# A hybrid decoder step on one core: a write-after-read order across two names of one SBUF stretch, VectorE for urgent GpSimd work, another order of the seven products of a pair, and two figures of the planner

## The chip, the core and the metric

The kernel runs on one core of one Trainium2 chip. The metric is the device time of one execution in microseconds. An execution of the kernel before takes 1107.15 us (median of three: 1103.31, 1107.15 and 1110.06).

## What is computed

Two decoder layers run over 512 prompt tokens and 8 sample tokens of 1024 channels. A layer is an input projection, three kinds of token mixing (window attention, a gated recurrence, causal pooling), an output projection with a residual and a LayerNorm, and then a feed-forward block with a residual and a second LayerNorm:

```
u = x @ w_in            # 1024 -> mixed widths, attention / recurrence / pooling
x = LayerNorm(alpha * x + concat(A, B, C) @ w_out)
x = LayerNorm(alpha * x + relu(x @ w_ff1)^2 @ w_ff2)     # 1024 -> 4096 -> 1024
```

The outputs are the last hidden states of both token groups and the updated caches.

## The kernel before

**Tiles.** The tokens are worked on in two halves: half A has 256 prompt tokens, half B has the other 256 and the 8 sample tokens (264 columns). Activations lie with channels on the partitions, in eight chunks `m` = 0 to 7 of 128 channels. Every float32 matmul is done as three matmuls on pieces of reduced width (hi by hi, lo by hi, hi by lo), so each operand has two tiles: `xh`, `xl` for the layer's input, `hh`, `hl` for the hidden values of the feed-forward block, and a high and a low half in each of the seven weight slots `w`. In the listings `xh_113`, `xl_115`, `hh_0_124`, `hl_0_125`, `y_0_92` are half A's, `xh_114`, `xl_116`, `hh_0_126`, `hl_0_127`, `y_0_94` half B's. A product of 128 output channels over 1024 inputs is 24 matmuls.

**Weights.** SyncE issues loads of 1 MB into two buffers `raw` in turn. Each holds the weights of two products. ScalarE casts the high half (`CAST w<-raw`), VectorE subtracts it to get the low half (`w<-raw,w`), and then the buffer may be loaded again. All waits of SyncE's loads are in the order of its queue.

**Planner.** The kernel text only records operations in a `Plan`; `Plan.order` (L225) then list-schedules all of them with estimated durations and due times (`rank`), and each engine issues its work in that order. An operation recorded with `either` (L338) may go to VectorE or GpSimd, decided in `pick` (L257): another engine than the first named takes it under the rules at L265 to L271. `cost` (L174) gives a load its bytes, and `dma_free` (L252) is the time from which the planner takes the DMA rings to be free. Dependences are by tile and region (`add`, L124). The framework below then puts in the semaphore waits, by its own view of which memory an instruction reads and writes.

**The shared stretch.** One stretch of SBUF, 8384 floats in each partition, is known by two names: `over_f` (float32) and `over_r` (the type for the matmuls), with `plan.alias` mapping the second to the first (L346 to L348). By `over_f` it holds rotating work lines of the attention and norm stages (`place`, L349), among them the zero-padded keys `KZ`, which two GpSimd memsets clear at the start of each layer (`layer_start`, L786), and the bias line of the last norm, loaded from `in_ln_b` (`Norm.prepare`, L1183). By `over_r` it holds the sums of input tiles T1 to T4 of the pairs, which fill the whole stretch.

**Feed-forward.** It runs in passes of eight hidden chunks: passes 0 to 3 for half A, 1 to 4 for half B. In a pass, `f1` products make hidden chunks (relu, square, `hh`, `hl`), then `f2` products add to the running sum `y`. Three chunk pairs of passes 2 and 3 and two of pass 1 are done for both halves together by `do_pair` (L1429): seven block products p1 to p7 of 12 matmuls each give two chunks for both halves, in place of eight; each reads T1 to T4 (`over_r`) or `xh`, `xl`, and goes to a PSUM bank `s`, `t` or `mm`. `close` makes a hidden tile from the finished sums: VectorE add into `ra`, VectorE relu and square into `rb`, ScalarE cast into `hh`, VectorE subtract into `hl`. The products are recorded in the order p1, p6, p7, p2, p4, p5, p3, and the tiles close in the order A m, A m+1, B m+1, B m. After the last pair of a pass come half A's `f2` products, then half B's; each reads all eight hidden tiles of its half, m = 7 last. There are six such ends of pair groups, three in each layer.

**Norms.** `Norm.chunk(m)` (L1206) runs as each chunk of `y` is finished: it adds the chunk to `acc` (chunks 3 and 7 name VectorE first, the others GpSimd), and after chunk 3 a matmul with `onesm` gives the shift (`x<-acc,onesm`), after chunk 7 the mean, by the same kind of matmul.

Of the kernel before, what the change touches and what calls it, by code (L numbers as in the profile page):

```python
# [19 lines left out]
ADD, SUB, MUL, MAX, MIN = ALU.add, ALU.subtract, ALU.mult, ALU.max, ALU.min  # L20
# [41 lines left out]
class Plan:  # L62
# [3 lines left out]
    def __init__(self, tc):  # L66
        self.tc = tc
        nc = tc.nc
        self.engs = {"V": nc.vector, "S": nc.scalar, "G": nc.gpsimd, "T": nc.tensor, "P": nc.sync}
        self.ops = []  # L70
        self.writes, self.reads = {}, {}
        self.rings, self.psum = {}, set()
        self.alias, self.large = {}, False


    def tile(self, pool, shape, dt, tag, bufs, name, psum=False):
# [47 lines left out]
    def add(self, first, *others):  # L124
# [19 lines left out]
        for a, w in [(a, False) for a in ins] + [(a, True) for a in outs]:  # L144
            nm = self.alias.get(a.name, a.name)
            if a.space == bass.MemoryType.DRAM:
                continue
            r = self.region(a)
            wl, rl = self.writes.setdefault(nm, []), self.reads.setdefault(nm, [])

            def hit(q):
                return q[0] < r[1] and r[0] < q[1] and any(x < d and c < y for x, y in q[2] for c, d in r[2])
            for q, o in wl:
                if hit(q):
                    deps.add(o)
            if w:
                for q, o in rl:
                    if hit(q):
                        deps.add(o)

                def inside(q):
                    return r[0] <= q[0] and q[1] <= r[1] and all(any(c <= x and y <= d for c, d in r[2]) for x, y in q[2])
                wl[:] = [x for x in wl if not inside(x[0])]
                rl[:] = [x for x in rl if not inside(x[0])]
                wl.append((r, op))
            else:
                if nm in self.psum:
                    deps.update(o for _, o in rl if o.eng != eng or len(o.alts) + len(op.alts) > 2)
                rl.append((r, op))
        deps.discard(op)  # L170
        op.deps = deps
        return op

    def cost(self, op, method, outs, ins, args, kw):  # L174
# [10 lines left out]
        if method == "dma_start":  # L185
            b = 4
            for k in out.shape:
                b *= k
            op.bytes = b
            op.dur = 1.0 if op.eng == "G" else 0.5  # L190
        elif op.eng == "T":
            if method == "transpose":
# [32 lines left out]
    def order(self):  # L225
# [23 lines left out]
            if not o.deps:  # L249
                release(o)  # L250
        free = {e: 0.0 for e in pool}
        cur_set, dma_free, late = None, 0.0, -nxt_pe  # L252
        held = {e: 0.0 for e in pool}
        other = {"V": "G", "G": "V"}
        done = []
# [1 line left out]
        def pick(e):  # L257
# [6 lines left out]
            for est, o in found:  # L264
                if est <= t + WINDOW or len(o.alts) > 1:  # L265
                    start = max(free[e], est)
                    if e != o.eng:
                        if e == "G":
                            if o.rank + late - start < o.alts[e][1] + MARGIN:
                                continue  # L270
                        elif max(free[o.eng], est) <= start + BUSY:  # L271
                            continue
                    if est > t + WINDOW:
                        continue
# [48 lines left out]
def trunk_kernel(ctx, tc, x_prompt, x_sample, cache_k, cache_v, state_h, state_conv, state_pool,  # L323
# [1105 lines left out]
    def do_pair(l, p, c):  # L1429
# [29 lines left out]
            V.tensor_tensor(lo[:, mm], q, hi[:, mm].bitcast(F32), SUB)  # L1459
        p1 = mul(0, wa, 0, xf, 0, 264, (j, "a"))  # L1460
        S.copy(out=e1, in_=p1)
        p6 = mul(1, wb, 4, sums["T2"], 0, 264, (j, "b"))
        V.tensor_tensor(u2, e1, p6, ADD)
        p7 = mul(0, wc, 0, sums["T3"], 0, 264, (j, "c"))
        V.tensor_tensor(u3, u2, p7, ADD)
        p2 = mul(2, wa, 4, xf, 4, 256, (j, "a"))
        close(0, m, 0, e1, p2)
        p4 = mul(1, wc, 4, sums["T4"], 0, 256, (j, "c"))
        close(0, m + 1, 1, u3, p4)
        p5 = mul(0, wb, 0, sums["T1"], 0, 264, (j, "b"))  # L1470
        close(1, m + 1, 1, u3, p5)
        t = line("ra0", 264, "fr")
        V.tensor_tensor(t, u2, p5, ADD)
        p3 = mul(2, wd, d0, (xh[1], xl[1]), 4, 264, dk)
        close(1, m, 0, t, p3)

    def do_f2(l, p, m, h):
        ps = product((l, "f2%d" % p, m // 2, m % 2), h, hid[h][0], hid[h][1])
# [147 lines left out]
```

## Time and profile before

The profiled execution took 1105.39 us, 0.2% under the median; its trace spans 1103.3 us, and 2.1 us lie around that.

| | |
|---|---|
| device time, median of three runs | 1107.15 us |
| profiled execution: device time, span | 1105.39 us, 1103.3 us |
| TensorE busy | 1075.4 us, 97% |
| VectorE / ScalarE / GpSimd busy | 796.4 / 552.4 / 209.6 us |
| HBM read | 112.72 MB |

In the profile, PE is TensorE's matmuls and PEld its weight loads, DVE is VectorE, ACT ScalarE, POOL GpSimd, SP and SPq SyncE and its DMA queue. Since the planner issues everything from one place, all instructions have the line L319; groups are told apart by operation and tile names. In a view by time, a row gives the start, the duration, the engine, the operation with its output and inputs, and in brackets the idle time before it with what ended that. Starts are counted from the span's start. A row "E a <- F b: t, n, max" of the waits says that engine E's instructions writing a waited t us in n waits for engine F's instruction writing b.

### The profile page before, as it was taken

The page shows a single profiled execution, that of the slowest core. Times are in us where ns is not written, and L with a number is a line of the kernel's source. Part 1 is how long each engine was busy: PE and PEld are TensorE (multiplying, and loading weights), DVE is VectorE, ACT ScalarE, POOL GpSimd, SP SyncE. Part 2 cuts the span into 40 slices and gives each one's busy share as a digit, 9 for nine tenths or more (in the row PEclk, how much of TensorE's full clock was granted, in tenths as well). Part 3 has the DMA queues.
Part 4 walks back from the last instruction along what each step waited for, and adds up shares of the span by engine and source line. Part 5 has one row for each costly group of instructions (what it writes and reads, how often), then busy time and mean ns, then how long its engine had stood idle before and what let it go on. Part 6 is the DMA issues. An engine that isn't in the chain of part 4 may idle for free.

```text
span 1103.3 us, 21246 instructions
## 1 busy us (share of the span) xinstructions
PE 1075.4 (97%) x8541; PEld 1046.6 (95%) x8541; DVE 796.4 (72%) x1661; ACT 552.4 (50%) x1066; POOL 209.6 (19%) x352
## 2 busy tenths in 40 slices
PE   8999999999999999999999999999999999989997
PEld 7988898999999999999998899999999999989996
DVE  5747769999559548669874596799975774675666
ACT  6658755755124224237476776566532431343343
POOL 4334334210000000022242443223000000002103
PEclk9999999999999999999999999999999999999999
DMA  9330413634313422434534040346242242242431
GB/s 266 98 76 3 114 44 116 192 120 137 111 60 98 132 77 78 124 106 155 172 89 99 1 116 5 115 144 205 77 128 67 75 153 77 78 134 83 148 116 40
DMA packets 120021, 116.58 MB, mean 106 GB/s; under 512 B 4481, under 2 KB 118171, under 8 KB 119875
## 3 DMA queue, kind: packets, MB, share of 16 engines
q1 hardware_dynamic: 119570, 115.16, 34.2%
q8 instruction: 67, 1.10, 0.4%
q14 instruction: 32, 0.25, 0.1%
q0 software_dynamic: 352, 0.06, 0.0%
HBM read 112.72 MB, written 4.84 MB: 107 GB/s over the span
## 4 chain that ended last, share of the span: by engine, by line
PE 80%; DVE 7%; ACT 5%; DMA 4%; issue 2%; SPq 1%; POOL 0%; DVEq 0%; ACTq 0%; POOLq 0%
PE mm L319 62%; PE s L319 9%; PE t L319 7%; PE x L319 2%; DVE y L319 2%; DVE over_f L319 2%; DMA raw<-in_w_ff_dram 2%; ACT L319 1%; DVE w L319 1%; DMA raw<-in_w_out_dram 1%; SPq L319 1%; ACT over_f L319 1%; ACT w L319 1%; DMA over_f<-in_x_sample_dram 1%; DVE ra L319 1%
## 5 line engine op out<-in xcount | busy, mean ns | idle before, releaser
L319 PE MATMUL mm<-hh,w 128*128 128x264 f32 (+1 forms) x2496 | 465.6, 285 | 0.8 <-ACT hh L319 0.8
L319 PE MATMUL mm<-xh,w 128*128 128x264 f32 (+1 forms) x2048 | 403.2, 290 | 1.0 <-ACT xh L319 0.9
L319 PEld LDWEIGHTS mm<-hh,w 128*128 128x128 f32 x2496 | 391.9, 190 | 2.8 <-ACT hh L319 1.4
L319 PE MATMUL mm<-hl,w 128*128 128x264 f32 (+1 forms) x1248 | 354.8, 285 | 0.4 <-DVE hl L319 0.4
L319 PEld LDWEIGHTS mm<-xh,w 128*128 128x128 f32 x2048 | 325.9, 190 | 7.1 <-issue 3.8
L319 ACT CAST w<-raw 128x1024 fp32r<-128x1024 f32 (+1 forms) x202 | 209.1, 1041 | 244.7 <-PE mm L319 204.8
L319 PE MATMUL mm<-xl,w 128*128 128x264 f32 (+1 forms) x1024 | 297.0, 290 | 0.0
L319 DVE TENSOR_TENSOR w<-raw,w 128x1024 fp32r<-128x1024 f32 (+1 forms) x202 | 247.5, 1231 | 56.6 <-ACT w L319 53.7
L319 PEld LDWEIGHTS mm<-hl,w 128*128 128x128 f32 x1248 | 237.2, 190 | 1.2 <-DVE hl L319 0.8
L319 PEld LDWEIGHTS mm<-xl,w 128*128 128x128 f32 x1024 | 194.2, 190 | 3.9 <-issue 3.4
L319 DVE TENSOR_TENSOR y<-y,mm 128x256 f32<-128x256 f32 (+1 forms) x96 | 40.5, 422 | 77.7 <-PE mm L319 77.4
L319 ACT CAST hh<-rb 128x264 fp32r<-128x264 f32 (+1 forms) x128 | 50.9, 410 | 54.6 <-DVE rb L319 54.3
L319 POOL TENSOR_SCALAR w<-four 128x512 fp32r<-128x512 f32 x4 | 2.6, 640 | 376.0 <-DVE four L319 376.0
L319 DVE TENSOR_TENSOR hl<-rb,hh 128x264 fp32r<-128x264 f32 (+1 forms) x128 | 52.4, 424 | 8.6 <-ACT hh L319 8.6
L319 PE MATMUL s<-over_r,w 128*128 128x264 f32 x384 | 53.0, 286 | 5.7 <-DMA over_f<-in_ln_b_dram 4.3
L319 PEld LDWEIGHTS s<-over_r,w 128*128 128x128 f32 x384 | 49.1, 189 | 6.3 <-DMA over_f<-in_ln_b_dram 4.6
L319 PE MATMUL t<-over_r,w 128*128 128x264 f32 (+1 forms) x384 | 51.1, 282 | 0.0
L319 PEld LDWEIGHTS t<-over_r,w 128*128 128x128 f32 x384 | 48.0, 188 | 0.0
L319 ACT CAST w<-four 128x1024 fp32r<-128x1024 f32 (+1 forms) x28 | 24.2, 866 | 41.2 <-PE mm L319 26.3
L319 ACT ACT_TABLE_LOAD x32 | 41.1, 1283 | 3.0 <-DVE nm L319 1.7
L319 ACT ACTIVATE over_f<-y 128x264 f32<-128x264 f32 (+1 forms) x49 | 19.4, 418 | 41.5 <-DVE y L319 30.0
L319 ACT ACTIVATE ra<-mm 128x256 f32<-128x256 f32 (+1 forms) x64 | 24.3, 384 | 29.9 <-PE mm L319 29.7
(288 smaller groups left out, 1346.7 us busy)
## 6 DMA issues: line engine op xcount, KB each, us to landing
raw<-in_w_ff_dram SPq DMA_DIRECT2D x80, 1024.0 KB
raw<-in_w_in_dram SPq DMA_DIRECT2D x7, 1024.0 KB
raw<-in_w_in_dram SPq DMA_DIRECT2D x8, 512.0 KB
raw<-in_w_out_dram SPq DMA_DIRECT2D x8, 512.0 KB
raw<-in_w_out_dram SPq DMA_DIRECT2D x16, 256.0 KB
y<-in_x_prompt_dram SPq DMA_DIRECT2D x4, 256.0 KB
raw<-in_w_in_dram SPq DMA_DIRECT2D x4, 256.0 KB
y<-in_x_prompt_dram SPq DMA_DIRECT2D x2, 512.0 KB
```

The lines of the kernel that those rows point to most:

```text
L319: o.ins = fn(*args, **kw)
```

## The change

Four things are changed in the text:

1. `Plan.add` remembers, in `second`, the last operation that touched the stretch by the alias `over_r`. Every later operation that writes it by its own name `over_f` is made to depend on that one, whichever region it writes.
2. In `cost`, a load whose tile has 64 partitions counts 1.75 times its bytes; in `order`, the rings are taken to be busy until 1.6 us. Both are figures of the planner, no instruction is changed by them.
3. In `pick`, VectorE may take an operation that names GpSimd first not only when GpSimd would start over 0.3 us later, but also when its due time is nearer than 3 us (`MARGIN`).
4. In `do_pair`, the products come in the order p1, p5, p6, p2, p7, p3, p4, with other banks, and the tiles close in the order A m, B m+1, B m, A m+1.

```diff
--- before.py
+++ after.py
@@ -71,6 +71,7 @@
         self.writes, self.reads = {}, {}
         self.rings, self.psum = {}, set()
         self.alias, self.large = {}, False
+        self.second = {}
 
 
     def tile(self, pool, shape, dt, tag, bufs, name, psum=False):
@@ -167,6 +168,10 @@
                 if nm in self.psum:
                     deps.update(o for _, o in rl if o.eng != eng or len(o.alts) + len(op.alts) > 2)
                 rl.append((r, op))
+            if a.name in self.alias:
+                self.second[nm] = op
+            elif w and nm in self.second:
+                deps.add(self.second[nm])
         deps.discard(op)
         op.deps = deps
         return op
@@ -186,7 +191,7 @@
             b = 4
             for k in out.shape:
                 b *= k
-            op.bytes = b
+            op.bytes = b * 1.75 if out.shape[0] == 64 else b
             op.dur = 1.0 if op.eng == "G" else 0.5
         elif op.eng == "T":
             if method == "transpose":
@@ -249,7 +254,7 @@
             if not o.deps:
                 release(o)
         free = {e: 0.0 for e in pool}
-        cur_set, dma_free, late = None, 0.0, -nxt_pe
+        cur_set, dma_free, late = None, 1.6, -nxt_pe
         held = {e: 0.0 for e in pool}
         other = {"V": "G", "G": "V"}
         done = []
@@ -268,7 +273,7 @@
                         if e == "G":
                             if o.rank + late - start < o.alts[e][1] + MARGIN:
                                 continue
-                        elif max(free[o.eng], est) <= start + BUSY:
+                        elif max(free[o.eng], est) <= start + BUSY and (e != "V" or o.rank + late - start > MARGIN):
                             continue
                     if est > t + WINDOW:
                         continue
@@ -1459,20 +1464,20 @@
             V.tensor_tensor(lo[:, mm], q, hi[:, mm].bitcast(F32), SUB)
         p1 = mul(0, wa, 0, xf, 0, 264, (j, "a"))
         S.copy(out=e1, in_=p1)
-        p6 = mul(1, wb, 4, sums["T2"], 0, 264, (j, "b"))
+        p5 = mul(1, wb, 0, sums["T1"], 0, 264, (j, "b"))
+        p6 = mul(0, wb, 4, sums["T2"], 0, 264, (j, "b"))
         V.tensor_tensor(u2, e1, p6, ADD)
-        p7 = mul(0, wc, 0, sums["T3"], 0, 264, (j, "c"))
-        V.tensor_tensor(u3, u2, p7, ADD)
         p2 = mul(2, wa, 4, xf, 4, 256, (j, "a"))
         close(0, m, 0, e1, p2)
-        p4 = mul(1, wc, 4, sums["T4"], 0, 256, (j, "c"))
-        close(0, m + 1, 1, u3, p4)
-        p5 = mul(0, wb, 0, sums["T1"], 0, 264, (j, "b"))
+        p7 = mul(1, wc, 0, sums["T3"], 0, 264, (j, "c"))
+        V.tensor_tensor(u3, u2, p7, ADD)
         close(1, m + 1, 1, u3, p5)
+        p3 = mul(2, wd, d0, (xh[1], xl[1]), 4, 264, dk)
         t = line("ra0", 264, "fr")
         V.tensor_tensor(t, u2, p5, ADD)
-        p3 = mul(2, wd, d0, (xh[1], xl[1]), 4, 264, dk)
         close(1, m, 0, t, p3)
+        p4 = mul(0, wc, 4, sums["T4"], 0, 256, (j, "c"))
+        close(0, m + 1, 1, u3, p4)
 
     def do_f2(l, p, m, h):
         ps = product((l, "f2%d" % p, m // 2, m % 2), h, hid[h][0], hid[h][1])
```

The matmuls and loads are the same in number. VectorE has 21 instructions more, ScalarE 5 fewer, GpSimd 16 fewer. Line numbers grow by 5, so L319 of the listings before is L324 after.

**TensorE, the last pair of the second layer, before.** The rows are the end of A's tile m, the T4 product into `t_122`, and p5 into `s_144`; what an instruction waits for by a semaphore stands in brackets (DMAHW5 is a DMA queue).

```order
L319 MATMUL mm_130<-xl_115,w_87 128x256
L319 MATMUL mm_130<-xh_113,w_87 128x256
L319 MATMUL t_122<-over_r,w_85 128x256 x12
L319 MATMUL s_144<-over_r,w_90 128x264 [waits Activation_49]
L319 MATMUL s_144<-over_r,w_90 128x264
L319 MATMUL s_144<-over_r,w_90 128x264 [waits DMAHW5_49]
L319 MATMUL s_144<-over_r,w_90 128x264 x9
L319 MATMUL mm_128<-xh_114,w_89 128x264
```

The same place after: the T4 product is now the last of the pair, into `s_144`, and half A's `f2` follows at once.

```order
L324 MATMUL mm_128<-xl_116,w_90 128x264
L324 MATMUL mm_128<-xh_114,w_90 128x264
L324 MATMUL s_144<-over_r,w_85 128x256 [waits Activation_49]
L324 MATMUL s_144<-over_r,w_85 128x256 x11
L324 MATMUL mm_129<-hh_0_124,w_84 128x256
L324 MATMUL mm_129<-hl_0_125,w_84 128x256
```

The wait of a matmul on `over_r` for a DMA queue is gone: the load of the bias line from `in_ln_b` now stands behind the last product that reads `over_r`. The same holds for two waits on GpSimd (its memsets of `KZ`) in the last pair of the first layer.

**VectorE, the end of the last pair, after.** `ra_0_151` from `s_143` is the sum of half A's tile 7, `rb_0_153` its square, `hl_0_125` its low half; `hl_0_127` and `ra_0_150` are half B's. Before, half A's two tiles were closed ahead of half B's.

```order
L324 TENSOR_TENSOR ra_0_151<-acc_157,s_144 128x256
L324 TENSOR_TENSOR hl_0_127<-rb_0_153,hh_0_126 128x264
L324 TENSOR_TENSOR ra_0_150<-ra_0_150,mm_128 128x264
L324 SCALAR_TENSOR_TENSOR rb_0_153<-ra_0_151 128x256
L324 SCALAR_TENSOR_TENSOR rb_0_152<-ra_0_150 128x264
L324 TENSOR_TENSOR w_90<-raw_93,w_90 128x1024
L324 TENSOR_TENSOR hl_0_125<-rb_0_153,hh_0_124 128x256
L324 TENSOR_TENSOR hl_0_127<-rb_0_152,hh_0_126 128x264
```

Before, at the same place:

```order
L319 TENSOR_TENSOR ra_0_151<-acc_157,t_122 128x256
L319 TENSOR_TENSOR hl_0_125<-rb_0_152,hh_0_124 128x256
L319 SCALAR_TENSOR_TENSOR rb_0_153<-ra_0_151 128x256
L319 TENSOR_TENSOR ra_0_150<-acc_156,s_144 128x264
L319 TENSOR_TENSOR ra_0_151<-acc_157,s_144 128x264
L319 TENSOR_TENSOR hl_0_125<-rb_0_153,hh_0_124 128x256
L319 TENSOR_TENSOR w_85<-raw_93,w_85 128x1024
L319 TENSOR_TENSOR ra_0_150<-ra_0_150,mm_128 128x264
```

What moved: the closing of half A's last tile went behind products p3 and p4, next to half B's, with a weight split between its square and its low half.

**VectorE, half B's first norm of the first layer.** Before, the last rows ahead of the mean; `y_0_94<-..._129` is chunk 7's residual, `acc_157<-acc_157,y_0_94` adds a chunk to the norm's sum.

```order
L319 TENSOR_TENSOR y_0_94<-mm_129,four 128x264
L319 TENSOR_TENSOR over_f<-over_f 128x264
L319 TENSOR_TENSOR w_88<-raw_93,w_88 128x1024
L319 TENSOR_TENSOR over_f<-over_f 128x264
L319 TENSOR_TENSOR w_89<-raw_95,w_89 128x1024
L319 TENSOR_TENSOR over_f<-over_f 128x264
L319 TENSOR_TENSOR acc_157<-acc_157,y_0_94 128x264
```

After:

```order
L324 TENSOR_TENSOR over_f<-over_f 128x264
L324 TENSOR_TENSOR xl_115<-over_f,xh_113 128x256
L324 SCALAR_TENSOR_TENSOR over_f<-y_0_92,pcol_98,over_f 128x256
L324 TENSOR_TENSOR y_0_94<-mm_129,four 128x264
L324 TENSOR_TENSOR acc_157<-acc_157,y_0_94 128x264
L324 SCALAR_TENSOR_TENSOR xl_115<-over_f,pcol_98,xh_113 128x256
```

What moved: the sum takes chunk 7 right behind its residual, and the low halves of five weight slots (`w_85` to `w_89`), which were made ahead of it, are now made behind it; two of the sums of chunks 4 to 6, which were GpSimd's, are VectorE's. On TensorE the shift's matmul went from the seventh chunk's product back into the product of chunk 4. The second layer changes in the same way.

## The prediction

> **What bounds the kernel now.** I read the page's busy shares and chain first, then TensorE's waits over the whole span, then the time around each large wait.
>
> ```profile
> span 1103.3 us, 21246 instructions
> PE 1075.4 (97%) x8541; PEld 1046.6 (95%) x8541; DVE 796.4 (72%) x1661; ACT 552.4 (50%) x1066; POOL 209.6 (19%) x352
> PE 80%; DVE 7%; ACT 5%; DMA 4%; issue 2%; SPq 1%; POOL 0%; DVEq 0%; ACTq 0%; POOLq 0%
> ```
>
> TensorE is busy 97% of the span, and no matmul is added or taken away. The most that any order can win is the 1103.3 − 1075.4 = 28 us in which it stands, and what it loses at a lower clock. So the question is which of these microseconds the change reaches, and which new ones it makes.
>
> ```profile
> PE x L319 <- DVE acc L319: 6.4, 5, 1.8
> PE s L319 <- DMA over_f<-in_ln_b_dram: 4.3, 1, 4.3
> PE t L319 <- DMA y<-in_x_prompt_dram: 3.6, 1, 3.6
> PE s L319 <- POOL over_f L319: 1.3, 2, 0.7
> ...
> PE mm L319 <- ACT hh L319: 0.8, 2, 0.4
> ...
> PE mm L319 <- DVE hl L319: 0.4, 2, 0.2
> ```
>
> The second and fourth row are strange: a matmul into `s` that waits for writes of `over_f`. The third row is the start of the program, which nothing here touches.
>
> **The shared stretch.** By time, the second row is in the last pair of layer 2:
>
> ```profile
> 982.34 1.58 PE L319 MATMUL t<-over_r,w 128*128 128x256 f32 x12
> 983.76 0.40 PE L319 MATMUL s<-over_r,w 128*128 128x264 f32 x2
> 988.50 1.72 PE L319 MATMUL s<-over_r,w 128*128 128x264 f32 x9 [4.34 <-DMA over_f<-in_ln_b_dram]
> ```
>
> ```profile
> 984.24 0.35 SPq L319 DMA_DIRECT2D over_f<-in_ln_b_dram  x1
> ```
>
> The product into `t` reads T4, at floats 6336 to 8384 of the stretch. The bias line lies at 6752 to 7808, inside T4, so its load rightly waits for T4's product. But the next product reads T1, from float 0 on, and waits for the bias's landing all the same: the framework takes the float32 write and the `over_r` read for a conflict without comparing regions. In the order after, T4's product is the last of the pair, and the new dependence puts the load behind it; no `over_r` matmul of this pair waits for a DMA any more. The gain is 4.34 us of waiting, and something behind it:
>
> ```profile
> 984.00:988.50 4.50, 0.16 (x2) 0.00 (x0) 1.73 (x4) 1.45 (x2) 0.00 (x0) 1.00 0.64 175
> 989.40:992.80 3.40, 3.40 (x17) 3.40 (x17) 2.24 (x4) 1.05 (x1) 0.00 (x0) 0.51 0.38 132
> 992.80:996.20 3.40, 3.40 (x31) 3.40 (x30) 2.57 (x5) 1.71 (x3) 0.00 (x0) 1.00 0.02 5
> ```
>
> The columns are the stretch, its length, busy time and count of PE, PEld, DVE, ACT and POOL, and then the granted clock. After the wait, one stretch of 3.4 us runs at a clock of 0.51: 17 matmuls where the next equal stretch has 31. The 14 missing ones at about 0.12 us are 1.7 us. Together 4.3 + 1.7 = **6.0 us**, and I see no reason for less unless the wait turns up elsewhere. The clock's part can be doubted. [...]
>
> ```profile
> 664.00:668.00 4.00, 2.88 (x21) 2.38 (x19) 3.36 (x13) 3.96 (x10) 1.16 (x2) 1.00 0.00 0
> 668.00:671.50 3.50, 3.50 (x16) 3.21 (x15) 2.40 (x5) 1.07 (x4) 1.40 (x4) 0.57 0.00 0
> ```
>
> Here PE is still busy for 2.88 of 4 us, and the clock falls to 0.57 in the next 3.5 us nevertheless. So gaps that add up to a microsecond can cost another 1.7, which I come back to among the rivals.
>
> The fourth row of the waits is the same thing in layer 1: the two memsets of `KZ` for the next layer, at floats 3616 to 4640.
>
> ```profile
> 443.96 0.52 POOL L319 MEMSET over_f<- 64x512 f32 x1 [22.27 <-PE s L319]
> ...
> 445.73 0.52 POOL L319 MEMSET over_f<- 64x512 f32 x1 [1.24 <-PE s L319]
> ```
>
> ```profile
> 444.54 1.13 PE L319 MATMUL s<-over_r,w 128*128 128x264 f32 x7 [0.70 <-POOL over_f L319]
> ...
> 446.30 0.64 PE L319 MATMUL s<-over_r,w 128*128 128x264 f32 x3 [0.63 <-POOL over_f L319]
> ```
>
> 0.70 + 0.63 = **1.3 us**, gone with the memsets behind the last product. What is late instead: the memsets and the bias line each come at most two products later (24 matmuls, 2.9 us). `KZ` is read in the next layer's attention, the bias in the last norm's store, both behind passes of `f2`, so I take nothing for that. On SyncE's queue the bias's load waits for PE with the weight loads behind it. It stands one weight load later in the queue, so the load behind it is late by 2.9 us less that place; the bound is 0 to 2.9, and I take 0.
>
> **The norm of half B, both layers.** The first row of the waits, and all of the `hh` and `hl` rows, lie mostly in two places. The same view cut to 170 to 215 us and to 705 to 750 us:
>
> ```profile
> PE x L319 <- DVE acc L319: 2.4, 2, 1.4
> PE mm L319 <- ACT hh L319: 0.4, 1, 0.4
> PE mm L319 <- DVE hl L319: 0.2, 1, 0.2
> ...
> PE x L319 <- DVE acc L319: 2.7, 2, 1.8
> ```
>
> The second stretch repeats the `hh` and `hl` rows with the same numbers, so the four places hold 2.4 + 2.7 + 2 × 0.6 = 6.3 us. Why the sum is late is seen ahead of the second wait:
>
> ```profile
> 188.01 0.94 POOL L319 TENSOR_TENSOR acc<-acc,y 128x264 f32<-128x264 f32 x1
> ...
> 188.27 1.77 DVE L319 TENSOR_TENSOR w<-raw,w 128x1024 fp32r<-128x1024 f32 x1
> ...
> 189.96 0.95 DVE L319 TENSOR_TENSOR over_f<-over_f 128x264 f32<-128x264 f32 x1
> 190.84 0.42 DVE L319 TENSOR_TENSOR acc<-acc,y 128x264 f32<-128x264 f32 x1
> 191.31 0.71 PE L319 MATMUL x<-acc,onesm 128*128 128x264 f32 x2 [1.40 <-DVE acc L319]
> ```
>
> The adds to `acc` are a chain. GpSimd's share of it takes 0.94 us a step where VectorE's takes 0.42, and VectorE does a weight split of 1.77 us before it adds chunk 7. In the order after, three of the five adds that were GpSimd's are VectorE's in this norm, the last add stands right behind chunk 7's residual, and the mean's matmul stands 19 matmuls (2.3 us) behind the end of chunk 7's product. Residual, add and their waits need about 0.42 + 0.42 + 0.5 = 1.3 us, less than 2.3. So the `acc` wait for the mean should vanish; the shift's matmul goes three products earlier, with only its neighbours' sum to wait for. I take the `acc` waits as gone, less a remainder of 0.6 in all, and of the `hh` and `hl` waits nothing: 5.1 − 0.6 = **4.5 us**. The bounds are 0 (the work that was ahead is merely put behind) and 6.3.
>
> The added cost is VectorE's: 21 instructions of at most 0.95 us over the whole program, 9 to 20 us on an engine that stands 28% of the span; it counts only in these two places. The price of the move is four weight splits in a row behind chunk 7's add (4 × 1.23 us by the row below), and so later weight buffers: the third rival.
>
> **The pairs' ends.** Now half A's tile 7 closes last, and `f2` of half A follows at once. In the trace such a close, of a tile that was not last, is:
>
> ```profile
> 348.96 0.41 DVE L319 TENSOR_TENSOR ra<-gq,mm 128x256 f32<-128x256 f32 x1
> 349.41 0.42 DVE L319 SCALAR_TENSOR_TENSOR rb<-ra 128x256 f32<-128x256 f32 x1
> ...
> 350.31 0.42 DVE L319 TENSOR_TENSOR hl<-rb,hh 128x256 fp32r<-128x256 f32 x1
> ...
> 354.44 1.22 DVE L319 TENSOR_TENSOR w<-raw,w 128x1024 fp32r<-128x1024 f32 x1
> ```
>
> ```profile
> 349.87 0.41 ACT L319 CAST hh<-rb 128x256 fp32r<-128x256 f32 x1 [1.55 <-DVE rb L319]
> ```
>
> From the start of `ra` to the end of `hh` it is 349.87 + 0.41 − 348.96 = 1.32 us, and 1.77 to the end of `hl`. In the order after, two other operations of half B (0.8 us) come between `ra` and `rb` of tile 7, and a split (1.2 us) before `hl`. With 0.5 us from the product's end to the start of `ra`, `hh` is there after 0.5 + 1.3 + 0.8 = 2.6 us and `hl` after 0.5 + 1.8 + 2.0 = 4.3. TensorE's order wants `hh` behind 21 or 22 matmuls of the first `f2` product, and `hl` 8 to 10 matmuls of the second later. By the chain's long row
>
> ```profile
> 273.50 56.59 PE mm L319 x471
> ```
>
> a matmul is 56.59 / 471 = 0.120 us, so that is at 2.5 and 3.6 us. The lack is 0.1 us for `hh` and, counted from there, some 0.6 for `hl`, of which TensorE has the rest of the second product in hand where the order allows. I take 0.4 us for each of the six ends, **2.4 us lost**, with 0 and 0.9 each (0 to 5.4) as bounds. The inner ends of a group, followed by a product that reads only inputs, cost nothing: its 12 matmuls are the cover, and without it an inner end would cost the same 0.4.
>
> **Planner's figures for loads.** They change no instruction, only places: a load that the planner takes to be later makes it give TensorE other work first. The weight loads of `w_out` and the start are where that could show. The orders of these two places are nearly the same before and after, so I take 0, with 0.5 to either side.
>
> **Sum.** Against the profiled execution: 1105.4 − 6.0 − 1.3 − 4.5 + 2.4 = 1096.0. The profiled execution is 1.8 us under the median of the runs shown, so the same sum against the median gives 1097.8. Of the small waits outside the named places (5 us in all by the list) the new order may gain or lose a microsecond or two. I say **1096**.
>
> **The rivals.**
>
> *A. Only the ordering pays.* VectorE is the nearest engine to full in the norm's stretch, and moved work meets it again: the norm gain is 0 and the pairs' ends cost the upper 5.4. Then 1105.4 − 7.3 + 5.4 = 1103.5; with the middle cost of 2.4 it is 1100.5, which I take for this case. For it: the operations beside GpSimd's took 0.95 us instead of 0.42 above, so VectorE is slower there than its work tells. Against it: GpSimd does fewer of them after.
>
> *B. Short gaps halve the clock.* Each of the six pairs' ends has two short waits, and by the 664 us rows above gaps of about 1 us in 4 were followed by 3.5 us at 0.57. If four of the six ends are followed by such a stretch (1.7 us), that is 6.8 more: 1103. Against it: at 188 to 192 us the wait of 1.40 was followed by no slow stretch, and the ends are otherwise dense.
>
> *C. Late weights, slower than before.* The place is pass 0 of the feed-forward block in each layer, where only half A runs and a 1 MB load serves 48 matmuls, 48 × 0.120 = 5.8 us, against
>
> ```profile
> 171.80 5.76 DMA raw<-in_w_ff_dram
> ```
>
> so a late load is never caught up within the pass. The low halves that empty the buffers now come behind half B's last sum, so the loads that began at 171.80 and 176.63 start some 6 and 9 us later.
>
> ```profile
> 176.63 0.37 SPq L319 DMA_DIRECT2D raw<-in_w_ff_dram  x1
> ...
> 187.50 12.51 SPq L319 DMA_DIRECT2D raw<-in_w_ff_dram  x3
> ```
>
> From 176.63 to the next at 187.50 the queue had nothing to start for 10.9 us, which is the cover. My count from the order gives each weight 2 to 5 us from its split to its first matmul. From a lateness of 5 us beyond that the mechanism takes more than the norm gave; if a whole load is missed, 5.8 us in each layer, and with the norm's 4.5 not won (TensorE stands there anyway): 1096 + 11.6 + 4.5 = 1112.
>
> *D. The change does not do what it says.* The new dependence is for the planner; should the framework still see a conflict with another write of `over_f`, the waits stay and only the pairs' cost comes: 1105.4 + 2.4 − 4.5 = 1103 with the norm gain, 1108 without. Against it: in the order after no `over_r` matmul of the two last pairs has such a wait.
>
> **How the numbers follow.** The forecast has 0.52, A 0.20, B 0.08, C 0.13, D 0.07. The forecast's own range is 1105.4 − 7.3 − 6.3 + 0 = 1092 at the best and 1105.4 − 7.3 − 2 + 5.4 = 1101.5 at the worst; a few microseconds of small waits widen the lower end to 1089. To leave out no more than 2 in 10 the range must take in A and B at 1103.5; I put **1088 to 1105**. About 0.5% (5.5 us) is what a measurement of this kernel can tell from no change, so faster means below 1101.6 and slower above 1112.7. Faster: 0.52 × 0.95 + A 0.20 × 0.65 + B 0.08 × 0.4 + C and D 0.02 = 0.68. Slower: C 0.13 × 0.45 and D 0.07 × 0.15 with 0.03 for what I have not seen: 0.10. The rest, 0.22, is the same.
>
> **What would show it.** In TensorE's waits after: no row from `over_f<-in_ln_b` and none from GpSimd's `over_f` to `s`, and a clock of 1.00 behind the last pair of layer 2 (the ordering's 7.3 us). The row `x <- acc` falls from 6.4 to about 2, the rest being the program's end. The `hh` and `hl` rows grow from 1.2 to some 3 us and lie at the six ends. A wait of matmuls for `w` or `raw` near 195 to 235 or 730 to 770 us would be C. The forecast is wrong if any of the first two stays, or if the `hh` and `hl` rows exceed 5 us.

## The result, and the profile after

The changed kernel takes 1093.81 us (median of five, 1092.89 to 1099.34), before 1107.15 us (median of five, 1103.31 to 1111.38). The ratio is 0.9894, with a 95% interval of 0.9867 to 0.9920. A second set of runs gave 1095.79 us and 0.9886 (0.9868 to 0.9904). It is faster by some 12 us; 1096 was forecast.

The profiled execution of the changed kernel is the slowest of the five, 1099.34 us with a span of 1097.5 us. That it shows only 5.8 us less than the profile before has a reason in the clock (a mean of 0.989 here, 0.995 in the profile before), told below. The page after has at its top:

```profile
span 1097.5 us, 21225 instructions
...
PE 1076.9 (98%) x8541; PEld 1049.7 (96%) x8541; DVE 797.9 (73%) x1682; ACT 549.7 (50%) x1061; POOL 190.2 (17%) x336
```

TensorE's waits after (total, times, longest):

```profile
PE t L324 <- DMA y<-in_x_prompt_dram: 4.4, 1, 4.4
PE mm L324 <- ACT hh L324: 3.2, 2, 1.6
...
PE x L324 <- ACT rb L324: 1.1, 1, 1.1
PE t L324 <- DVE over_f L324: 1.1, 2, 0.6
...
PE mm L324 <- DVE hl L324: 0.9, 2, 0.5
```

Three rows of before are gone: the bias's load (4.3), GpSimd's `over_f` (1.3) and VectorE's `acc` (6.4, of which 1.1 is left as `x <- rb` at the program's end). The rows for `hh` and `hl` have grown, from 0.8 to 3.2 and from 0.4 to 0.9. The first row, at the program's start, differs from execution to execution: it is 4.4 here and 3.6 in the second profile of the same kernel.

The place of the longest wait, the last pair of layer 2, now reads so on TensorE and on SyncE:

```profile
982.17 1.62 PE L324 MATMUL t<-over_r,w 128*128 128x264 f32 x12
...
985.08 1.58 PE L324 MATMUL s<-over_r,w 128*128 128x256 f32 x12
986.50 0.28 PE L324 MATMUL mm<-hh,w 128*128 128x256 f32 x1
```

```profile
986.74 0.35 SPq L324 DMA_DIRECT2D over_f<-in_ln_b_dram  x1
```

The bias's load is issued when the T4 product is done, and no product waits for it. The two stretches that had 2 and 17 matmuls before have 40 and 31 now, at full clock (columns as before):

```profile
984.00:988.50 4.50, 4.50 (x40) 4.50 (x39) 4.50 (x12) 2.55 (x5) 0.00 (x0) 1.00 0.86 275
989.40:992.80 3.40, 3.40 (x31) 3.40 (x30) 2.70 (x6) 0.49 (x1) 0.00 (x0) 1.00 0.60 161
```

In layer 1 the two memsets of `KZ` follow the last product that reads the stretch:

```profile
450.67 1.09 POOL L324 MEMSET over_f<- 64x512 f32 x2 [29.27 <-PE s L324]
```

**How the time of a run is split here.** Each run has a span and a mean granted clock. Their product is taken, as an estimate, for the time that the run would take at full clock, and the rest counts as lost to the clock. For the kernel before, over the 20 runs beside the first four experiments, the span goes with the clock (correlation −0.83): runs at 0.986 to 0.987 have spans of 1107.8 to 1112.0 us, runs at 0.995 to 0.996 of 1101.8 to 1103.6. Span times clock is 1096.7 us in the mean there, with 1.7 us of spread (1093.4 to 1099.2), where the spans reach over 10.2 us. This product counts only as a reckoning: a wait at half clock is counted as lost too. The sets of runs come from different chips, so kernels of different sets are compared by the ratio and by these differences. The table has means over all runs of a kernel, and in brackets the difference to the kernel before in the same set of runs. A difference of less than about 1 us in the column of span times clock is within the spread.

| kernel | median us | ratio to before, 95% | span × clock | lost to the clock |
|---|---|---|---|---|
| full change | 1093.81 | 0.9894 (0.9867 to 0.9920) | 1086.5 | 6.6 |
| full change, second set | 1095.79 | 0.9886 (0.9868 to 0.9904) | 1086.9 (−8.6) | 7.1 (−3.5) |
| part 1: dependence alone | 1098.27 | 0.9897 (0.9861 to 0.9933) | 1091.2 (−5.5) | 4.9 (−4.9) |
| part 4: pairs' order alone | 1101.03 | 0.9939 (0.9910 to 0.9968) | 1094.1 (−2.6) | 5.7 (−4.1) |
| part 3: urgent work alone | 1105.47 | 0.9973 (0.9948 to 0.9997) | 1092.9 (−3.8) | 11.3 (+1.5) |
| part 2: load figures alone | 1103.42 | 0.9953 (0.9937 to 0.9969) | 1094.4 (−1.1) | 6.9 (−3.7) |
| parts 1 and 4 | 1099.10 | 0.9907 (0.9877 to 0.9937) | 1091.9 (−4.8) | 5.3 (−4.5) |
| parts 1 to 3 | 1094.42 | 0.9876 (0.9840 to 0.9913) | 1086.6 (−9.9) | 5.5 (−2.6) |
| parts 1, 3, 4 | 1099.35 | 0.9931 (0.9903 to 0.9959) | 1088.2 (−8.3) | 9.0 (+0.9) |
| full, hidden tiles due earlier | 1091.82 | 0.9859 (0.9828 to 0.9890) | 1086.4 (−10.1) | 3.5 (−4.6) |
| full, all TensorE inputs earlier | 1087.53 | 0.9821 (0.9784 to 0.9858) | 1082.6 (−13.9) | 3.3 (−4.8) |
| the same with the old pairs | 1088.14 | 0.9818 (0.9799 to 0.9836) | 1082.8 (−12.7) | 3.3 (−7.3) |

### The profile page after: what moved, and what is told of

It reads as the page before. It is cut to its first block, busy times and chain, and to the rows that moved or that the text cites. A ratio compares the mean times of both kernels' runs of the same rounds, so it can differ in the third digit from the quotient of the medians.

```text
span 1097.5 us, 21225 instructions
## 1 busy us (share of the span) xinstructions
PE 1076.9 (98%) x8541; PEld 1049.7 (96%) x8541; DVE 797.9 (73%) x1682; ACT 549.7 (50%) x1061; POOL 190.2 (17%) x336
## 4 chain that ended last, share of the span: by engine, by line
PE 80%; DVE 8%; ACT 5%; DMA 3%; issue 1%; SPq 1%; DVEq 0%; ACTq 0%
PE mm L324 64%; PE s L324 8%; PE t L324 7%; DVE w L324 2%; PE x L324 2%; ACT L324 2%; DMA raw<-in_w_out_dram 2%; DVE over_f L324 1%; DMA raw<-in_w_ff_dram 1%; SPq L324 1%; DVE y L324 1%; ACT over_f L324 1%; ACT w L324 1%; DVE rb L324 1%; DVE hl L324 1%
## 5 line engine op out<-in xcount | busy, mean ns | idle before, releaser
L324 PE MATMUL mm<-hh,w 128*128 128x264 f32 (+1 forms) x2496 | 469.9, 287 | 3.2 <-ACT hh L324 3.2
L324 PE MATMUL mm<-xh,w 128*128 128x264 f32 (+1 forms) x2048 | 399.8, 289 | 1.1 <-ACT xh L324 1.1
L324 PEld LDWEIGHTS mm<-hh,w 128*128 128x128 f32 x2496 | 395.0, 192 | 5.2 <-ACT hh L324 3.8
L324 PE MATMUL mm<-hl,w 128*128 128x264 f32 (+1 forms) x1248 | 356.4, 287 | 0.9 <-DVE hl L324 0.9
L324 ACT CAST w<-raw 128x1024 fp32r<-128x1024 f32 (+1 forms) x202 | 208.3, 1040 | 265.0 <-PE mm L324 195.9
L324 PEld LDWEIGHTS mm<-xh,w 128*128 128x128 f32 x2048 | 323.7, 189 | 6.9 <-issue 3.8
L324 PE MATMUL mm<-xl,w 128*128 128x264 f32 (+1 forms) x1024 | 296.1, 289 | 0.0
L324 DVE TENSOR_TENSOR w<-raw,w 128x1024 fp32r<-128x1024 f32 (+1 forms) x201 | 249.3, 1249 | 53.0 <-ACT w L324 51.6
L324 PEld LDWEIGHTS mm<-hl,w 128*128 128x128 f32 x1248 | 239.2, 192 | 1.8 <-DVE hl L324 1.3
L324 PEld LDWEIGHTS mm<-xl,w 128*128 128x128 f32 x1024 | 193.3, 189 | 4.1 <-issue 3.4
L324 DVE TENSOR_TENSOR y<-y,mm 128x256 f32<-128x256 f32 (+1 forms) x96 | 40.5, 422 | 79.8 <-PE mm L324 79.7
L324 ACT CAST hh<-rb 128x264 fp32r<-128x264 f32 (+1 forms) x128 | 51.1, 408 | 55.6 <-DVE rb L324 55.1
L324 POOL TENSOR_SCALAR w<-four 128x512 fp32r<-128x512 f32 x6 | 3.9, 651 | 375.4 <-DVE four L324 322.0
L324 DVE TENSOR_TENSOR hl<-rb,hh 128x256 fp32r<-128x256 f32 (+1 forms) x128 | 53.3, 430 | 9.2 <-ACT hh L324 9.1
L324 PE MATMUL t<-over_r,w 128*128 128x264 f32 x384 | 51.8, 284 | 0.0
L324 PE MATMUL s<-over_r,w 128*128 128x264 f32 (+1 forms) x384 | 51.1, 282 | 0.0
L324 PEld LDWEIGHTS t<-over_r,w 128*128 128x128 f32 x384 | 48.7, 188 | 0.0
L324 PEld LDWEIGHTS s<-over_r,w 128*128 128x128 f32 x384 | 48.2, 188 | 0.0
L324 ACT ACTIVATE ra<-mm 128x256 f32<-128x256 f32 (+1 forms) x64 | 24.5, 382 | 36.3 <-PE mm L324 36.3
L324 ACT CAST w<-four 128x1024 fp32r<-128x1024 f32 (+1 forms) x26 | 23.0, 885 | 38.1 <-PE mm L324 27.7
L324 DVE TENSOR_TENSOR w<-four,w 128x1024 fp32r<-128x1024 f32 (+1 forms) x32 | 30.5, 953 | 10.9 <-ACT w L324 10.7
```

Source lines behind the costliest of these rows:

```text
L324: o.ins = fn(*args, **kw)
```

## The experiments

**Part 1 alone.** Edit, against the kernel before:

```diff
+            if a.name in self.alias:
+                self.second[nm] = op
+            elif w and nm in self.second:
+                deps.add(self.second[nm])
```

> Only the new dependence over the stretch (part 1); VectorE's order is row for row that of before. Theory (the ordering alone frees the two waits of matmuls on over_r, 1.3 and 4.3 us, and the slow stretch of 1.7 us): 7.3 us less, about 1100, and no row of TensorE's waits names over_f from the bias's load or from GpSimd. Rival (the waits were cover, and the weight loads queued behind the bias's load come late instead): 1104 to 1107, with the lost time in matmuls waiting for w.

Measured 1098.27 us, ratio 0.9897. By the names in the profile, every engine's instructions come in the order of before, but for one load of SyncE, so this is the price of the two waits alone. Of TensorE's waits, the two of the stretch are gone, and the norm's waits of `x` still add up to 6.4 us:

```profile
PE x L324 <- DVE acc L324: 5.4, 4, 2.0
PE t L324 <- DMA y<-in_x_prompt_dram: 3.6, 1, 3.6
PE mm L324 <- ACT xh L324: 1.7, 1, 1.7
...
PE x L324 <- ACT w L324: 1.0, 1, 1.0
```

The row that names `w` is no new wait: it stands at 178.31 us with 0.99 us, where before, at 178.50, 0.98 us were put down to `acc`. No product waits for its weights, so the two waits were not cover. At full clock 5.5 us are won, which is the 1.3 + 4.3 of the two rows; but 4.9 us less are lost to the clock, where the sum had 1.7. In the profile before, two slow stretches behind gaps lie ahead of the program's end (0.57 from 668 us, 0.51 from 989.4 us); in this one the clock is 1.00 up to 1084 us.

**Part 4 alone.** Edit:

```diff
-        p6 = mul(1, wb, 4, sums["T2"], 0, 264, (j, "b"))
+        p5 = mul(1, wb, 0, sums["T1"], 0, 264, (j, "b"))
+        p6 = mul(0, wb, 4, sums["T2"], 0, 264, (j, "b"))
...
+        p4 = mul(0, wc, 4, sums["T4"], 0, 256, (j, "c"))
+        close(0, m + 1, 1, u3, p4)
```

> Only the new order of the seven products and of the closes (part 4). In its order the bias's load stands behind the T4 product, now the last, so that wait goes; the two memsets stay ahead of an over_r product. The prediction's terms: 6.0 us won, 2.4 lost at the six ends of groups: 1103.5. Rival 1 (the ends cost nothing, as the trace after has no wait there): 1101. Rival 2 (ends at their upper bound of 0.9 each): 1106.5.

Measured 1101.03 us, which is rival 1's figure. The bias's wait is gone with the order alone, since its region is T4's; the memsets still cost one wait, and `hh` and `hl` together have grown from 1.2 to the 2.1 of `hl`:

```profile
PE mm L319 <- DVE hl L319: 2.1, 3, 0.7
...
PE t L319 <- POOL over_f L319: 0.6, 1, 0.6
```

At full clock it wins 2.6 us, less than the 4.3 of the bias's wait; in the profiled execution 1.6 us of the difference stands at the program's start (`xh`, 2.5 us against 0.9), which differs between runs of one kernel (1.1 and 1.9 us in the two profiles of the full change).

**Parts 1 and 4.** The edits of the two runs above together.

> Parts 1 and 4 together, without the urgent work and the load figures. If the ends of the groups cost nothing and the ordering is worth 7.3 us, the same as the dependence alone, about 1100; if the ends cost what the prediction took, 1102.3. Rival (the pairs' order has a gain of its own, work for TensorE at the groups' starts): below 1098.

Measured 1099.10 us, ratio 0.9907, against 0.9897 for the dependence alone: no gain of the pairs' order, and a cost of 0.7 us at full clock within a spread of 0.8. Its waits at all six ends together are one of 0.6 us, where the prediction had 2.4. In the view from 760 to 1070 us, with none at the ends in the view from 225 to 560 us:

```profile
PE mm L324 <- DVE hl L324: 0.6, 1, 0.6
```

The full change has in the same two views only this:

```profile
PE mm L324 <- DVE hl L324: 0.3, 1, 0.3
```

**Part 3 alone.** Edit:

```diff
-                        elif max(free[o.eng], est) <= start + BUSY:
+                        elif max(free[o.eng], est) <= start + BUSY and (e != "V" or o.rank + late - start > MARGIN):
```

> Only VectorE's right to urgent work of GpSimd (part 3). Its order in half B's first norm, with the mean's matmul 19 matmuls behind chunk 7, is that of the full change. The prediction's term: 4.5 us less, 1102.6. What the trace after shows (the waits for acc gone, one wait of 1.6 us for hh at the start of f2 in each layer): some 3 us less, 1104. Rival (the norm's gain needs the load figures too): 1107.

Measured 1105.47 us, ratio 0.9973: 3.0 us, with an interval from 0.3 to 5.8. The norm's gain needs no other part. At full clock it is 3.8 us, nearer to the prediction than the time is; 1.5 us more than before are lost to the clock. The waits show what was exchanged:

```profile
PE s L319 <- DMA over_f<-in_ln_b_dram: 3.7, 1, 3.7
PE mm L319 <- ACT hh L319: 3.2, 2, 1.6
```

The 6.4 us for `acc` are gone (1.1 is left as `x <- rb`), and `hh` costs 3.2 in place of 0.8. What holds `hh` up is read from VectorE and ScalarE of the full change, where the same wait stands at 209.40 us, at the start of half A's `f2` in pass 0:

```profile
205.68 1.21 DVE L324 TENSOR_TENSOR w<-raw,w 128x1024 fp32r<-128x1024 f32 x1
206.82 0.41 DVE L324 TENSOR_TENSOR hl<-rb,hh 128x256 fp32r<-128x256 f32 x1
207.15 0.76 DVE L324 TENSOR_TENSOR y<-y,four 128x264 f32<-128x264 f32 x2
207.84 0.96 DVE L324 TENSOR_TENSOR rb<-ra 128x256 f32<-128x256 f32 x1
```

```profile
207.41 0.38 ACT L324 ACTIVATE ra<-mm 128x256 f32<-128x256 f32 x1
...
208.63 0.42 ACT L324 CAST xh<-y 128x264 fp32r<-128x264 f32 x1
208.94 0.41 ACT L324 CAST hh<-rb 128x256 fp32r<-128x256 f32 x1
```

```profile
209.40 0.79 PE L324 MATMUL mm<-hh,w 128*128 128x256 f32 x2 [1.62 <-ACT hh L324]
```

The last `f1` product ends at 204.47, and `hh` of hidden tile 7 is there at 209.35, 4.9 us later. ScalarE takes the sum out of PSUM (`ra<-mm`) only at 207.41. VectorE's square (`rb`) follows at 207.84, behind two splits and half B's own norm (`y<-y,four`), and takes 0.96 us, with GpSimd at work from 206.65 to 208.53. Before, the same way took 3.0 us (207.69 to 210.66), with these steps:

```profile
207.84 0.37 ACT L319 ACTIVATE ra<-mm 128x256 f32<-128x256 f32 x1
```

```profile
209.24 0.98 DVE L319 TENSOR_TENSOR rb<-ra 128x256 f32<-128x256 f32 x1
```

Two splits stood ahead of the square there too (2.35 us from 206.97), so they are not what is new. New is half B's norm: its mean's matmul comes at 182.83 us in place of 191.31, and the rest of the norm now falls among the closes of the hidden tiles, on ScalarE and on VectorE. A late load adds to it:

```profile
197.25 1.23 DVE L324 TENSOR_TENSOR w<-raw,w 128x1024 fp32r<-128x1024 f32 x1 [1.10 <-ACT w L324]
```

VectorE stands 1.10 us for a cast that ScalarE starts at 196.17, after waiting 1.15 us for a load of `raw`. From there to the square VectorE has no idle time. In layer 2 it stands 0.53 us in the same way, and before the change in neither layer. So the work moved away from one wait came back at the next one. How much of the 1.62 us is the norm's work and how much the late load, no run separates.

**The full change without part 4, and without part 2.** The edit of that part is undone, the other three stay.

> The full change without its new order of products and closes (parts 1 to 3 only). If the pairs' order is worth nothing beside the dependence, as the runs of the dependence alone and of dependence with pairs say: the same as the full change, ratio to before 0.989 within 0.004. If the closes' order costs what the prediction took (2.4 us): ratio 0.987. Rival (the pairs' order carries a gain of its own): 0.992 or more.

> The full change without the two load figures (part 2). Prediction: nothing, ratio 0.989. Rival (the figures order the start and the w_out loads better): 0.992 or more.

With the old pairs 0.9876 and 1086.6 us at full clock: the pairs' order is worth nothing measurable beside the dependence. Without the figures 0.9931. That is past the rival's bound of 0.992, though the interval still overlaps with the full change's; so the figures were run alone.

**Part 2 alone.** Edit:

```diff
-            op.bytes = b
+            op.bytes = b * 1.75 if out.shape[0] == 64 else b
...
-        cur_set, dma_free, late = None, 0.0, -nxt_pe
+        cur_set, dma_free, late = None, 1.6, -nxt_pe
```

> Only the two load figures (part 2). From the run without them (span times clock 1.7 us more than the full change): 1 to 2 us less in span times clock than before, which shows as 1105 to 1106 us. The prediction took 0 within 0.5. Rival (the figures help only beside the urgent work): 1107, and span times clock as before.

Measured 1103.42 us, ratio 0.9953 (0.9937 to 0.9969): 5.2 us less, 3.4 to 7.0. Two numbers that no instruction uses win about as much as the urgent work does; the intervals overlap. At full clock it is 1.1 us, as expected, within a spread of about as much; 3.7 us less are lost to the clock. In its waits the row for `t` from VectorE's `over_f` (1.7 us before, at 131 and 666 us, in the last stage before the output projection) is gone; the row for `gq` at these places (1.0 us in two waits) is as before. By the names in the profile, from 60 us on all engines' orders are those of before, but for one exchange on ScalarE in each layer. Before, in layer 2:

```profile
658.10 1.05 ACT L319 CAST w<-raw 128x1024 fp32r<-128x1024 f32 x1 [1.37 <-DMA raw<-in_w_out_dram]
659.06 0.53 ACT L319 ACTIVATE four<-rb,sp 128x288 f32<-128x288 f32 x1
```

and with the figures:

```profile
656.02 0.56 ACT L319 ACTIVATE four<-rb,sp 128x288 f32<-128x288 f32 x1
...
657.29 1.05 ACT L319 CAST w<-raw 128x1024 fp32r<-128x1024 f32 x1 [0.71 <-DMA raw<-in_w_out_dram]
```

The activation, behind which ScalarE comes to the chain of `over_f`, no longer stands behind a cast that waits for a load of `w_out`. The full change has the same exchange in both layers, and the profile without the figures has not. What the clock did behind gaps at these places is looked at next.

**The full change again.**

> The full change once more, beside the two runs below. Theory (the spread of one kernel's runs is the granted clock: span times mean clock hardly changes from run to run, 1086.5 us for the full change and 1096.6 for before): span times clock again 1086.5 within 1, a clock of 0.99 to 0.996, and the slow stretches lie behind the waits at 208 and 746 us and near 666 us or not, by the run. Rival (the clock follows the program's place): the same slow stretches as in the first profile, that of 10 us behind 666 us too.

Span times clock came again at 1086.9 us, and the slow stretches are in other places. Around 131 us, in the windows view of this second profile (the column before the last two is the clock):

```profile
131.00:134.30 3.30, 2.26 (x14) 1.62 (x13) 2.79 (x12) 2.91 (x6) 1.26 (x2) 1.00 0.01 2
134.30:137.70 3.40, 3.40 (x17) 3.10 (x15) 2.14 (x6) 1.35 (x4) 0.85 (x3) 0.50 0.00 0
137.70:141.10 3.40, 3.40 (x17) 3.40 (x17) 0.60 (x3) 2.54 (x5) 0.00 (x0) 0.50 0.00 0
141.10:144.50 3.40, 3.40 (x18) 3.40 (x18) 1.29 (x5) 1.37 (x2) 0.00 (x0) 0.50 0.00 0
```

and in the first profile of the same kernel:

```profile
131.00:134.30 3.30, 2.25 (x14) 1.60 (x13) 3.05 (x12) 3.11 (x7) 0.91 (x1) 1.00 0.01 2
134.30:137.70 3.40, 3.40 (x29) 3.30 (x29) 2.36 (x6) 2.19 (x5) 1.22 (x3) 1.00 0.00 0
```

The same matmuls and the same gaps (PE busy for 2.26 and 2.25 of 3.3 us) were followed by 10.2 us at a clock of 0.50 in the one execution, some 5 us lost, and by none in the other. The first profile has its slow stretches behind the `hh` waits (0.50 from 210 to 212 and from 746 to 748 us) and near 666 us (0.50 from 668 to 676 us); the second has the same `hh` waits of 1.62 us and a clock of 1.00 behind both, here the one at 743 us:

```profile
742.00:746.00 4.00, 2.61 (x19) 2.41 (x20) 4.00 (x4) 2.09 (x6) 3.41 (x4) 1.00 0.74 255
746.00:750.00 4.00, 4.00 (x36) 4.00 (x35) 4.00 (x7) 3.16 (x6) 1.74 (x2) 1.00 0.56 157
```

The first profile has there:

```profile
742.00:746.00 4.00, 2.38 (x15) 2.07 (x14) 4.00 (x8) 3.21 (x7) 3.40 (x3) 0.85 0.65 208
746.00:750.00 4.00, 4.00 (x27) 4.00 (x27) 3.39 (x7) 2.83 (x5) 2.35 (x2) 0.73 0.38 106
```

So gaps of 1.0 us in 3.3 and of 1.6 in 4 were each followed by a lower clock in one of these two profiles, with 1.7 to 5 us lost, and by full clock in the other. The rival, that the clock follows the place, falls.

**The full change with hidden tiles due earlier.** Edits, against the full change. The first three lines make this run; the next run has 1.5 in place of 2.0, and the last four lines too:

```diff
+        op.pad = 2.0 if out.name[:2] in ("hh", "hl") else 0.0
...
-        return LATENCY.get(a.eng + eng, 0.2)
+        return LATENCY.get(a.eng + eng, 0.2) + (a.pad if eng == "T" else 0.0)
...
-           "VT": 0.15, "ST": 0.16
+           "VT": 0.35, "ST": 0.36
...
-LATE = 0.6
+LATE = 1.0
```

> The full change, and the planner counts 2.0 us more from the writing of hh or hl to its reading by TensorE, so that a hidden tile is due earlier and TensorE's order puts other products' matmuls ahead of the last tile's. Theory (the full change's remaining loss is the wait for hh at the start of f2 in each layer, 2.1 us with hl, and the slow stretch of 1.7 us behind it): those four waits vanish from TensorE's list and the clock stays at 1.00 near 208 and 746 us; some 5 to 7 us less than the full change, ratio 0.983 to 0.985. Rival (VectorE has too much to do there in any order): the wait comes back for another tile or for w, ratio 0.989.

> As the run before, with 1.5 us for hh and hl, 0.2 us more from any VectorE or ScalarE write to TensorE's read, and small matmuls released 1.0 in place of 0.6 us after their inputs. Theory: beside the four waits, those for over_f and gq near 141 and 673 us (1.3 us each in the full change) get shorter, and the slow stretch behind 666 us goes: ratio 0.980 to 0.984. Rival (small matmuls come too late and the attention's and recurrence's chains get longer): 0.99 or more.

The first took 1091.82 us, ratio 0.9859: half of what was expected. Its waits:

```profile
PE mm L325 <- ACT hh L325: 2.4, 2, 1.3
PE mm L325 <- DVE y L325: 1.6, 2, 0.8
PE x L325 <- DVE acc L325: 1.3, 1, 1.3
```

The `hh` waits are smaller but not gone, and others came in place of the rest, as the rival said; at full clock nothing is won (1086.4 us). What is won is 3 us of clock: its four runs have 0.996 to 0.997, and its profile has no slow stretch ahead of 1078 us. The second took 1087.53 us, ratio 0.9821, and beats both kernels. Its waits for `hh`, `hl`, `acc`, `gq` and `over_f` are gone; beside the program's start and end are left

```profile
PE mm L325 <- DVE xl L325: 1.6, 3, 0.6
...
PE s L325 <- ACT y L325: 0.6, 1, 0.6
PE mm L325 <- DVE y L325: 0.5, 1, 0.5
```

It wins another 4 us at full clock and 3 of the clock against the full change. With the old pairs' order the same figures give the same time:

> The faster version with the old order of products and closes (parts 1 to 3, and the planner's longer figures to TensorE's reads). If the pairs' order is worth nothing: as with the new order, ratio 0.982, span times clock 1082.6. If the old closes leave TensorE more ready work at the ends of groups now that the figures use it: 0.5 to 2 us less; if the new order was what let the figures work: 1086.

Measured 1088.14 us, ratio 0.9818.

## Why the prediction was right, and where it was not

**The shared stretch: right in the waits, too small in the clock.** The rows' 4.3 + 1.3 us are the 5.5 us that the dependence alone wins at full clock. That a slow stretch goes with its wait was the author's estimate. The runs bear it out here: behind the bias's wait the clock is 0.51 in the profile before (989.4 to 992.8 us), 0.63 and 0.52 with part 3 alone (990 to 994 us) and 0.50 with part 2 alone (984 to 990 us), and in the ten profiles without that wait it is 1.00 from 978 to 998 us. But the term of 1.7 us for the clock was mis-sized: the runs lost 4.9 us less to it. It was read from one execution, and the two profiles of the full change show how far one execution can differ from the next: 0.50 from 668 to 676 us in the first, from 134.3 to 144.5 us in the second.

**Half B's norm: the direction right, one step wrong.** The `acc` waits went as the 19 matmuls behind chunk 7 said. The step that failed is "of the `hh` and `hl` waits nothing": they grew from 1.2 to 4.1 us, where half B's norm, now earlier, and a late load hold up the close of the last hidden tile; this is read from the trace, and no run varied it by itself. The term was 4.5; part 3 alone measures 3.8 at full clock and 3.0 in all. The lateness of the loads was foreseen at some 6 and 9 us and is 6.1 and 9.7 (177.88 and 186.31 us in place of 171.80 and 176.63), but its price was looked for in TensorE's waits for `w` and `raw` (rival C) and not at the close of tile 7. The sign "some 3 us at the six ends" for these rows came near in size by luck: 4.1 us, nearly all of it in another place.

**The pairs' ends: wrong, nothing instead of 2.4 us.** The chain had two operations of half B in it at full price, and 0.5 us from the product's end to `ra`. In the trace after:

```profile
986.70 0.42 DVE L324 TENSOR_TENSOR ra<-acc,s 128x256 f32<-128x256 f32 x1
...
987.73 0.76 DVE L324 SCALAR_TENSOR_TENSOR rb<-ra 128x256 f32<-128x256 f32 x2
988.40 1.22 DVE L324 TENSOR_TENSOR w<-raw,w 128x1024 fp32r<-128x1024 f32 x1
989.54 0.76 DVE L324 TENSOR_TENSOR hl<-rb,hh 128x256 fp32r<-128x256 f32 x2
```

`ra` reads `s_144`, the T4 product's bank, and not `s_143`, as the text ahead of its listing has it. It starts 0.2 us after the next product's start (986.50), the independent operations on VectorE here start some 0.34 us apart (986.70, 987.04, 987.39, 987.73) and not 0.42, and `rb` of tile 7 starts 1.0 us after its `ra`, which holds the two others. With ScalarE's cast from 988.18, `hh` is there 2.1 us after that start, ahead of the 2.5 at which it is wanted, and the first of the two `hl` some 3.4 to 3.8, about the 3.6. Each step of my chain was a few tenths too long, which is all that the forecast of 0.4 an end was made of.

**The load figures: wrong, 5.2 us alone instead of 0.** The step was that the orders at the start and at the `w_out` loads are nearly the same. They are nearly the same, but the exchange on ScalarE ahead of a `w_out` cast took away the waits of 1.7 us in the thinnest stretch of the program. That the 3.7 us of clock come from there too is likely and not shown. Beside the other parts the figures are worth 1.7 us at full clock (1088.2 against 1086.5) and 2.4 of clock.

**The sum.** 9.4 us were forecast: 7.7 of waits and 1.7 of clock. Measured are 8.6 us at full clock and 3.5 of clock in the second set; the first set's 1086.5 is 10.1 under the 1096.6 that the kernel before has in the mean of the first two sets of experiments. The parts' gains at full clock add up to about that (5.5 + 3.8 + 1.1 = 10.4), those of the clock do not (4.9 + 3.7 − 1.5 = 7.1 against 3.5); one reading, which no run tests, is that a slow stretch can be lost only once, and that the `hh` waits of part 3 bring two new places for it. The errors do not cancel: the pairs' ends (2.4), the figures (1.1) and the clock (1.8) all made the forecast too slow, and only the norm (0.7) made it too fast. That 1096 is nevertheless 2.2 us from the median is luck of the base: the profiled execution was 1.8 us under the median of before, from which the same sum gives 1097.8, 4.0 us too much. The worst end of the range takes the norm at 2 us and not at its own bound of 0; with 0 it is 1103.5, which is still inside 1105.

**The rivals.** A: the ordering was not all, the norm paid too. B: short gaps were followed by a lower clock, but not at the pairs' ends, which have no gaps to speak of (0.3 us in all); it was 0.50 behind the `hh` waits and behind 666 us in the one profile of the full change, and behind 131 us in the other. C: the loads did come late, and the lateness reached ScalarE and VectorE, as told at part 3. No product waits for `w` or `raw` in any profile; the price is a share of the `hh` waits, at most the 1.10 and 0.53 us that VectorE stood for late casts in the two layers, and not 5.8 us a layer. D: the waits went in the order and in the trace.

## What to carry to other kernels

When two names share memory, look for a wait whose writer's region the reader does not touch, and move the writer behind the last reader under the other name: a plain order won as much here as all the rest. Work taken from ahead of one wait, and work that may now start earlier, has to be followed to the next reader on the same engines, which may be another stage's tile. And where one execution's clock moves by more than the effect, compare span times clock and the loss apart; the planner's latencies to the bounding engine, set 0.2 to 1.7 us longer, were worth another 6 to 8 us on top of the moves.

## What the hardware showed that was not expected

TensorE's lower clock cost 3 to 11 us of 1100 in the mean of a kernel's runs (3.3 to 11.3 in the table), and most of the spread between runs of one kernel went with it (correlation −0.83 between span and clock); the clock fell behind gaps far shorter than the 4.3 us wait. Gaps of 0.55 and 0.49 us in a stretch of small matmuls (PE busy 2.26 of 3.3 us) were followed by three stretches of 3.4 us at 0.50 in one execution, and gaps of 0.56 and 0.48 us at the same place by none in another. Why the clock stayed low for three stretches there, and for one behind the 4.3 us wait (0.51 for 3.4 us), the runs leave open. Whether the length of a gap decides is open too: no run varied one gap by itself.
